# First feed-forward of a streaming-encoder block: token scalings in two steps, one plain feature tile instead of two, last middles stored from GpSimd's queue

## Chip, cores and metric

The kernel runs on one core of a Trainium2 chip. The metric is the device time of one execution in microseconds (us), smaller is better. The engines are named as in the profile: PE (TensorE matmuls), PEld (its weight loads), DVE (VectorE), ACT (ScalarE), POOL (GpSimd), SP (SyncE, which here only issues DMAs). "SPq", "ACTq" and "POOLq" are DMA issues on those engines' queues.

## What is computed

One encoder block over 16 meta tokens and 1024 frames (1040 tokens, 1024 model features, 2816 hidden features), in float32:

```python
def swiglu(x, w_gate, w_up, w_down):
    return (jax.nn.silu(x @ w_gate) * (x @ w_up)) @ w_down

h = jnp.concatenate([meta, x], axis=1)
h = h + 0.5 * swiglu(rmsnorm(h, ffn1_norm[l]), ffn1_w_gate[l], ffn1_w_up[l], ffn1_w_down[l])
u = rmsnorm(h, mix_norm[l])          # one projection, attention and gated linear attention, merge
h = h + mixed @ w_out[l]
h = h + 0.5 * swiglu(rmsnorm(h, ffn2_norm[l]), ffn2_w_gate[l], ffn2_w_up[l], ffn2_w_down[l])
return rmsnorm(h, final_norm)[:, N_META:]
```

The change touches the first feed-forward (the first line that updates `h`) and, in one helper, both.

## The kernel before

**Arithmetic.** Every float32 product is made of three matmuls over halves: each operand is cut into a rounded high half (an ACT copy) and the remainder as low half (a DVE subtraction), and high·high, high·low and low·high are accumulated in PSUM. `halves` (L228, L229) makes such a pair.

**Tokens.** The 1040 tokens stand as two halves c = 0 and 1 of 520 columns, each of two chunks; chunks q = 0 to 3 are 256, 264, 256 and 264 columns wide. Tokens are transposed on PE tile by tile (`xps`, L554 and L556), eight tiles m per chunk. Chunks 0 and 1 are put as they are, without the row scale 1/rms, which isn't known yet. For chunks 2 and 3 `second_put` copies the transposed tile out (ACT L581, `xr`, stored to DRAM for the residual), scales it (DVE L582, a scalar_tensor_tensor into `ub`), makes its high half (ACT L583) and, one put later, its low half (DVE L585). `rescale(m)` (L590) scales tile m of the first token half afterwards and makes its halves anew.

**Hidden features.** There are 22 tiles of 128 hidden features. Tiles 20 and 21 are made first, chunk by chunk (`head_products`, L631 to L633: 16 steps of three matmuls), while tokens arrive and are put. The order of this part is written by hand: `hooks[q, f]` names what stands between the steps of chunk q and head f, a step number before each. `out_of(f, q)` (`head_out`, L648 to L653) is SiLU times up of a head, in two pieces; `later` runs pieces that were set aside in `behind`. Then features 0 and 1 are made in the same plain way (`more`, 4 chunks x 16 steps x 3 = 192 matmuls each), with `finish` (L740, L741) as their SiLU times up. Meanwhile DVE makes the differences of tokens (`token_sums`, L246 to L252) and their halves, which the other features need. Features 2 to 19 go through `gate_ups`: a seven-product scheme for 2x2 blocks, 7 x 4 x 3 x 2 = 168 matmuls of 260 columns per tile (L453). A tile takes its seven combined results to DRAM (`f1mid`) with `keep` (L237 to L240): a cast to the high half `kh`, a subtraction to the low half `kl`, and a store of each.

**Down.** `down` runs the seven products over `f1mid`: it loads its moving tiles with `load_t` (L346, the first 14 from SP's queue, the others from ACT's), weights with `load_weights` (L358, SP), makes weight sums on POOL (`sums`, L436) and adds results up (ACT L395, DVE L340). The last tile's seven `keep`s are not needed at once and are taken one at a time during the first products of `down` (`pump`). There, with `self.ending` set, `kh` and `kl` lie in the ring `tmp` of four buffers, so a third pair waits until the first has been stored, the fourth for the second, and so on. The second feed-forward has the same code, and only two such `keep`s.

**Queues.** Engines run their own instructions in order; a DMA that is issued from an engine's queue stands in that order too. PSUM has eight banks for the plain products, two to a chunk (`pg`, `pu`); a chunk can start when the two banks are free again.

Of the kernel before, what the change touches and what calls it, by code (L numbers as in the profile page):

```python
# [8 lines left out]
F32 = mybir.dt.float32  # L9
# [10 lines left out]
KT = D // P  # L20
# [4 lines left out]
NF = DFF // P  # L25
# [10 lines left out]
def hybrid_kernel(  # L36
# [4 lines left out]
    nc = tc.nc  # L41
# [58 lines left out]
    def split(hi, lo, src):  # L100
        nc.scalar.copy(hi, src)
        nc.vector.tensor_sub(lo, src, hi.bitcast(F32))
# [49 lines left out]
    LAST = 2  # L152
# [16 lines left out]
    class Seven:  # L169
# [65 lines left out]
        def keep(self, dst, src):  # L235
            hi, lo = [ttile(x, F32R, self.n) if self.ending else self.block(x, F32R) for x in ("kh", "kl")]
            nc.scalar.copy(hi, src)  # L237
            nc.vector.tensor_sub(lo, src, hi.bitcast(F32))
            nc.sync.dma_start(out=dst[:, 0:self.n], in_=hi.bitcast(F32))
            nc.sync.dma_start(out=dst[:, self.n:], in_=lo.bitcast(F32))  # L240

        def token_sums(self, ub, between=None):

# [215 lines left out]
    N1 = T // 2  # L459
# [21 lines left out]
    ffn1 = Seven("f1", N1, acc1, (t_a, t_b, blk, s_pool, w_ext), ffn1_w_gate, ffn1_w_up, ffn1_w_down)  # L481
# [48 lines left out]
    B = [[None] * KT, [None] * KT]  # L530
# [44 lines left out]
    def second_put(q, m, ps):  # L575
        c, c0, n = CH[q]
        if c0 == 0:
            ub[1][m], B[1][m] = ffn1.block("ub"), ffn1.operand(False, "tb")
        raw = s_pool.tile([P, WB], F32, tag="s", name="xr")[:, 0:n]
        u, hi = ub[1][m][:, c0:c0 + n], B[1][m][:, c0:c0 + n]  # L580
        nc.scalar.copy(raw, ps)  # L581
        nc.vector.scalar_tensor_tensor(u, ps, vec[:, G1 + m:G1 + m + 1], racc[:, N1 + c0:N1 + c0 + n], op0=ALU.mult, op1=ALU.mult)  # L582
        nc.scalar.copy(hi, u)  # L583
        nc.sync.dma_start(out=x_dram[1, m, :, c0:c0 + n], in_=raw)
        return lambda: nc.vector.tensor_sub(B[1][m][:, N1 + c0:N1 + c0 + n], u, hi.bitcast(F32))  # L585

    def rescale(m):

        u = ub[0][m]
        nc.vector.scalar_tensor_tensor(u, u, vec[:, G1 + m:G1 + m + 1], racc[:, 0:N1], op0=ALU.mult, op1=ALU.mult)  # L590
        ffn1.halves(B[0][m], u)

    dgs = {}

# [25 lines left out]
    def head_products(q, ws, hooks, both=False):  # L620

        c, c0, n = CH[q]
        pss = [bank(x)[:, 0:n] for x in ("pg", "pu")]
        at = 0
        for i, k in [(i, k) for k in range(KT) for i in range(2)] if both else [(i, k) for i in range(2) for k in range(KT)]:
            for go in hooks.get(at, ()):
                go()
            at += 1
            wh, wl = [w[:, k * P:(k + 1) * P] for w in ws[i]]
            xh, xl = B[c][k][:, c0:c0 + n], B[c][k][:, N1 + c0:N1 + c0 + n]  # L630
            nc.tensor.matmul(pss[i], wh, xh, start=(k == 0), stop=False)  # L631
            nc.tensor.matmul(pss[i], wh, xl, start=False, stop=False)
            nc.tensor.matmul(pss[i], wl, xh, start=False, stop=(k == KT - 1))  # L633
        return pss
# [38 lines left out]
    def later():  # L673
        while behind:
            behind.pop(0)()
# [12 lines left out]
    def do(fn, *a, **k):  # L688
        return lambda: fn(*a, **k)
# [4 lines left out]
    def out_of(f, q):  # L694
        def go():
            rest = head_out(f, q, done.pop((f, q), None))
            later()
            behind.append(rest)
        return go

    turned = [turn_x(0, m) for m in range(KT)]
    for m in range(KT):
        first_put(0, m, turned[m])
        if m in (0, 3):
# [10 lines left out]
                 **{8 + m: [put(2, m)] for m in range(KT)}},  # L715
        (2, 0): {2: [emptied(1, 1)], 3: [out_of(0, 0)], **{4 + m: [put(3, m)] for m in range(KT)}, 13: [out_of(1, 0)]},
        (2, 1): {0: [out_of(0, 1)], 2: [out_of(1, 1)], 4: [out_of(0, 2)], 6: [later],
                 **{8 + m: [do(rescale, m)] for m in range(KT)}},
        (3, 0): {4: [out_of(1, 2)], 5: [later]},
        (3, 1): {4: [out_of(0, 3)], 5: [later]},  # L720
    }
    for q in range(4):
        for f in range(LAST):
            done[f, q] = head_products(q, heads[f], hooks[q, f], f == 0)
    manual.__exit__(None, None, None)
    ffn1.tops.update(B11=B[0][0:4], B21=B[0][4:8], B12=B[1][0:4], B22=B[1][4:8])
    out_c, ends = [[None] * 2 for _ in range(2)], []

    def more(f):

        ws = [ffn1.plain_weights(cols_view(w, f * P)) for w in (ffn1_w_gate, ffn1_w_up)]
        for q in (2, 3, 0, 1):
            c, c0, n = CH[q]
            pss = head_products(q, ws, {})

            def finish(c=c, c0=c0, n=n, pss=pss):
                a = ttile("a")[:, 0:n]
                if c0 == 0:
                    out_c[f][c] = ffn1.block("m0")
                nc.scalar.activation(a, pss[0], AF.Silu)  # L740
                nc.vector.tensor_mul(out_c[f][c][:, c0:c0 + n], pss[1], a)  # L741
            ends.append(finish)

    def between(n, k):
        for _ in range(2 if (n, k) in (("T2", 3), ("T1", 3), ("T3", 3), ("T4", 3)) else 0):
            ends.pop(0)()

    more(0)
    out_of(1, 3)()
    later()  # L750
    more(1)
    ffn1.token_sums(ub, between)
    turn_rest()
    for f in range(2):
        ffn1.middle(f, *out_c[f])
    ps_singles.close()
    dbl.update(down=False, a=ExitStack(), b=ExitStack())
    dbl["pools"] = [dbl[x].enter_context(tc.tile_pool(name=f"psd{x}", bufs=1, space=PSUM, side=side))
                    for x, side in (("a", "right"), ("b", "left"))]
    ffn1.gate_ups(range(2, NF - LAST))  # L760
    dbl["down"] = True
    ffn1.down(x_dram)
    mids, ws = ffn1.load_last(True)
# [66 lines left out]
    for c in range(2):  # L830
# [3 lines left out]
        for m in range(KT):  # L834
# [4 lines left out]
            n = 0  # L839
# [942 lines left out]
```

## Time and profile before

| | us |
|---|---|
| median of 3 runs | 2033.24 (2032.82 to 2035.1) |
| the profiled execution | 2034.17 |
| its span in the trace | 2032.5 |
| PE busy in it | 1999.0 |
| DVE / ACT / POOL busy in it | 1400.4 / 882.1 / 178.2 |

The span is what the trace shows from the first instruction to the last; the profiled execution's own time is 1.7 us more. Start times in the rows are counted from the span's start. A line of the trace's order of time has start, duration, engine, line, operation, output and inputs, and in square brackets how long the engine was idle before it and what ended that. In tables of stretches, PEclk is the granted TensorE clock as a share of full speed (1.00 is 2.4 GHz, 0.50 is 1.2 GHz).

### The profile page before, as it was taken

The page shows a single profiled execution, that of the slowest core. Times are in us where ns is not written, and L with a number is a line of the kernel's source. Part 1 is how long each engine was busy: PE and PEld are TensorE (multiplying, and loading weights), DVE is VectorE, ACT ScalarE, POOL GpSimd, SP SyncE. Part 2 cuts the span into 40 slices and gives each one's busy share as a digit, 9 for nine tenths or more (in the row PEclk, how much of TensorE's full clock was granted, in tenths as well). Part 3 has the DMA queues.
Part 4 walks back from the last instruction along what each step waited for, and adds up shares of the span by engine and source line. Part 5 has one row for each costly group of instructions (what it writes and reads, how often), then busy time and mean ns, then how long its engine had stood idle before and what let it go on. Part 6 is the DMA issues. An engine that isn't in the chain of part 4 may idle for free. (4 is left out here: it accounts for less than half of the span.)

```text
span 2032.5 us, 32056 instructions
## 1 busy us (share of the span) xinstructions
PE 1999.0 (98%) x12084; PEld 1776.5 (87%) x12084; DVE 1400.4 (69%) x2441; ACT 882.1 (43%) x1722; POOL 178.2 (9%) x205
## 2 busy tenths in 40 slices
PE   8899999999999999999999999999999999999998
PEld 8799999999899988888888767888888888878888
DVE  5866677667578776566367667568767767757885
ACT  5534444444322255465366535345444544442222
POOL 1000000001232100003200000110000000023212
PEclk9899999999999999999999999999999999999999
DMA  6324345438977143346222555741544544599722
GB/s 205 111 90 144 124 147 178 137 118 330 347 288 272 49 159 102 115 153 201 56 61 66 188 175 184 252 140 44 197 138 134 188 135 135 202 376 356 279 92 84
DMA packets 285772, 343.06 MB, mean 169 GB/s; under 512 B 26406, under 2 KB 192032, under 8 KB 285616
## 3 DMA queue, kind: packets, MB, share of 16 engines
q1 hardware_dynamic: 267968, 279.60, 41.5%
q10 hardware_dynamic: 17296, 61.29, 8.0%
q8 instruction: 95, 1.56, 0.3%
q14 instruction: 61, 0.50, 0.1%
q0 software_dynamic: 352, 0.11, 0.1%
HBM read 220.66 MB, written 120.27 MB: 168 GB/s over the span
## 5 line engine op out<-in xcount | busy, mean ns | idle before, releaser
L453 PE MATMUL pb<-tt,wop 128*128 128x260 f32 (+1 forms) x2208 | 383.9, 327 | 0.0
L453 PEld LDWEIGHTS pb<-tt,wop 128*128 128x128 f32 x2208 | 330.9, 188 | 35.5
L229 DVE TENSOR_TENSOR wop<-s,wop 128x512 fp32r<-128x512 f32 x264 | 186.8, 709 | 118.3 <-ACT wop L228 117.5
L228 ACT CAST wop<-s 128x512 fp32r<-128x512 f32 x264 | 163.7, 621 | 232.0 <-PE pb L453 96.0
L453 PE MATMUL pb<-tm,wop 128*128 128x260 f32 (+1 forms) x1440 | 235.9, 320 | 5.5 <-DVE h L340 3.3
L453 PEld LDWEIGHTS pb<-tm,wop 128*128 128x128 f32 x1440 | 208.6, 190 | 25.1 <-DVE h L340 3.7
L228 ACT CAST wop<-raw 128x512 fp32r<-128x512 f32 x198 | 122.9, 621 | 221.5 <-PE pb L453 108.3
L229 DVE TENSOR_TENSOR wop<-raw,wop 128x512 fp32r<-128x512 f32 x198 | 140.2, 710 | 30.1 <-ACT wop L228 29.8
L453 PE MATMUL pd<-tt,wop 128*128 128x260 f32 (+1 forms) x768 | 135.1, 329 | 0.0
L436 POOL TENSOR_TENSOR s<-raw 128x512 f32<-128x512 f32 x28 | 37.0, 1322 | 1054.6 <-DMA tm<-f1mid 455.1
L453 PEld LDWEIGHTS pd<-tt,wop 128*128 128x128 f32 x768 | 115.9, 188 | 13.1
L340 DVE SCALAR_TENSOR_TENSOR h<-pb,h 128x520 f32<-128x520 f32 (+1 forms) x136 | 93.9, 693 | 40.1 <-PE pb L453 38.0
L453 PE MATMUL pd<-tm,wop 128*128 128x260 f32 (+1 forms) x720 | 118.8, 319 | 0.0
L453 PE MATMUL pb<-tb,wop 128*128 128x260 f32 (+1 forms) x672 | 112.3, 320 | 0.5 <-ACT vec L87 0.5
L453 PEld LDWEIGHTS pd<-tm,wop 128*128 128x128 f32 x720 | 104.3, 188 | 9.3
L453 PE MATMUL pd<-tb,wop 128*128 128x260 f32 (+1 forms) x672 | 112.2, 320 | 0.0
L453 PE MATMUL pa<-tb,wop 128*128 128x260 f32 (+1 forms) x672 | 112.0, 320 | 0.0
L453 PEld LDWEIGHTS pb<-tb,wop 128*128 128x128 f32 x672 | 97.9, 188 | 9.9 <-ACT vec L87 0.6
L453 PEld LDWEIGHTS pd<-tb,wop 128*128 128x128 f32 x672 | 97.9, 188 | 9.3
L453 PEld LDWEIGHTS pa<-tb,wop 128*128 128x128 f32 x672 | 97.8, 188 | 9.3
L436 DVE TENSOR_TENSOR s<-raw 128x512 f32<-128x512 f32 x90 | 61.9, 688 | 54.6 <-DMA raw<-in_ffn_w_up 52.9
L340 DVE SCALAR_TENSOR_TENSOR h<-pd,h 128x520 f32<-128x520 f32 (+3 forms) x112 | 72.7, 655 | 33.3 <-PE pd L453 17.5
(410 smaller groups left out, 4036.8 us busy)
## 6 DMA issues: line engine op xcount, KB each, us to landing
tm<-f1mid ACTq DMA_DIRECT2D x56, 520.0 KB, 6.1
tm<-f2mid ACTq DMA_DIRECT2D x56, 512.0 KB, 6.0
raw<-in_ffn_w_gate SPq DMA_DIRECT2D x42, 512.0 KB, 3.8
raw<-in_ffn_w_up SPq DMA_DIRECT2D x42, 512.0 KB, 4.2
raw<-in_ffn_w_down SPq DMA_DIRECT2D x80, 256.0 KB, 5.2
f1mid<-kh SPq DMA_DIRECT2D x70, 260.0 KB, 3.2
f1mid<-kl SPq DMA_DIRECT2D x70, 260.0 KB, 3.4
f2mid<-kh SPq DMA_DIRECT2D x70, 256.0 KB, 2.9
```

The lines of the kernel that those rows point to most:

```text
L228: nc.scalar.copy(x[:, 0:n], src)
L229: nc.vector.tensor_sub(x[:, n:2 * n], src, x[:, 0:n].bitcast(F32))
L340: nc.vector.scalar_tensor_tensor(hm, ps, 0.5, hm, op0=ALU.mult, op1=ALU.add)
L436: (eng.tensor_add if add else eng.tensor_sub)(a[s], a[x], a[y])
L453: nc.tensor.matmul(ps, y, z[:, s0:s0 + sn], start=(first and k == 0 and at == 0), stop=(at == 2 and k == len(cols) - 1), skip_group_check= ...
```

## The change

It does four things.

1. `second_put` sets both halves of a scaled tile aside (`split` makes the pair), where before only the low one was. They run behind the next tile's copy and scaling.
2. `rescale` sets its halves aside too, and its eight calls are spread: four with two steps between them in chunk 2's second head, four with three steps between them in chunk 3's first head, with `out_of(1, 2)` ahead of these.
3. One tile of features goes the plain way, not two; features 1 to 19 go through the seven products. `out_of(1, 3)` and its second piece stand inside the plain tile, `finish` of a chunk is called at other places of `token_sums`.
4. While `ending` is set, `keep` issues its two stores from GpSimd's queue, not from SP's. In the first feed-forward that is 14 stores, in the second 4.

```diff
@@ keep
-            nc.sync.dma_start(out=dst[:, 0:self.n], in_=hi.bitcast(F32))
-            nc.sync.dma_start(out=dst[:, self.n:], in_=lo.bitcast(F32))
+            eng = nc.gpsimd if self.ending else nc.sync
+            eng.dma_start(out=dst[:, 0:self.n], in_=hi.bitcast(F32))
+            eng.dma_start(out=dst[:, self.n:], in_=lo.bitcast(F32))
@@ second_put
-        nc.scalar.copy(hi, u)
         nc.sync.dma_start(out=x_dram[1, m, :, c0:c0 + n], in_=raw)
-        return lambda: nc.vector.tensor_sub(B[1][m][:, N1 + c0:N1 + c0 + n], u, hi.bitcast(F32))
+        return lambda: split(hi, B[1][m][:, N1 + c0:N1 + c0 + n], u)
@@ rescale
-        ffn1.halves(B[0][m], u)
+        later()
+        behind.append(lambda: ffn1.halves(B[0][m], u))
@@ hooks
         (2, 1): {0: [out_of(0, 1)], 2: [out_of(1, 1)], 4: [out_of(0, 2)], 6: [later],
-                 **{8 + m: [do(rescale, m)] for m in range(KT)}},
-        (3, 0): {4: [out_of(1, 2)], 5: [later]},
-        (3, 1): {4: [out_of(0, 3)], 5: [later]},
+                 **{8 + 2 * m: [do(rescale, m)] for m in range(4)}},
+        (3, 0): {4: [out_of(1, 2)], **{6 + 3 * i: [do(rescale, 4 + i)] for i in range(4)}},
+        (3, 1): {0: [later], 4: [out_of(0, 3)], 5: [later]},
@@ more, between
-            pss = head_products(q, ws, {})
+            pss = head_products(q, ws, hooks if q == 2 else {})
-        for _ in range(2 if (n, k) in (("T2", 3), ("T1", 3), ("T3", 3), ("T4", 3)) else 0):
+        if (n, k) in (("T2", 1), ("T2", 3), ("T1", 3), ("T3", 3)):
             ends.pop(0)()
-    more(0)
-    out_of(1, 3)()
-    later()
-    more(1)
+    more(0, {4: [out_of(1, 3)], 5: [later]})
     ffn1.token_sums(ub, between)
-    for f in range(2):
-        ffn1.middle(f, *out_c[f])
+    ffn1.middle(0, *out_c)
-    ffn1.gate_ups(range(2, NF - LAST))
+    ffn1.gate_ups(range(1, NF - LAST))
```

The order on ACT where chunk 3 is put. Before (`xr` is the copy out of PSUM, `tb` a high half; tiles m follow one another):

```order
L581 COPY xr_683<-xps_679 128x264
L583 CAST tb_552<-ub_551 128x264
L652 CAST kept_116<-a_672 128x256
L581 COPY xr_697<-xps_693 128x264
L583 CAST tb_565<-ub_564 128x264
```

In the changed kernel, the same place:

```order
L582 COPY xr_683<-xps_679 128x264
L653 CAST kept_116<-a_671 128x256
L582 COPY xr_696<-xps_692 128x264
L101 CAST tb_552<-ub_551 128x264
L582 COPY xr_709<-xps_705 128x264
L101 CAST tb_564<-ub_563 128x264
```

The cast of tile m (`tb_552`) stood ahead of the copy of tile m+1 and now stands behind it.

The order on DVE at the end of the rescalings. Before (`a_907` is SiLU times up of head 1, chunk 2, `out_of(1, 2)`; `ub_230` and `ub_235` are tiles 6 and 7 of the first token half; L246 to L248 are token differences):

```order
L590 SCALAR_TENSOR_TENSOR ub_230<-ub_230,vec_84,racc_115 128x520
L248 TENSOR_TENSOR ub_620<-ub_620,ub_201 128x520
L246 TENSOR_TENSOR ub_206<-ub_578,ub_206 128x520
L229 TENSOR_TENSOR tb_231<-ub_230,tb_231 128x520
L590 SCALAR_TENSOR_TENSOR ub_235<-ub_235,vec_84,racc_115 128x520
L247 TENSOR_TENSOR ub_578<-ub_634,ub_578 128x520
L246 TENSOR_TENSOR ub_211<-ub_592,ub_211 128x520
L229 TENSOR_TENSOR tb_236<-ub_235,tb_236 128x520
L649 TENSOR_TENSOR a_907<-pu_801,a_907 128x256
```

In the changed kernel (`a_893` is the same SiLU times up, `ub_211` is tile 3, `ub_220` tile 4):

```order
L590 SCALAR_TENSOR_TENSOR ub_211<-ub_211,vec_84,racc_115 128x520
L229 TENSOR_TENSOR tb_207<-ub_206,tb_207 128x520
L650 TENSOR_TENSOR a_893<-pu_801,a_893 128x256
L229 TENSOR_TENSOR tb_212<-ub_211,tb_212 128x520
L590 SCALAR_TENSOR_TENSOR ub_220<-ub_220,vec_84,racc_115 128x520
L654 TENSOR_TENSOR kept_119<-a_893,kept_119 128x256
L590 SCALAR_TENSOR_TENSOR ub_225<-ub_225,vec_84,racc_115 128x520
```

The reading of chunk 2's banks for head 1 (`pu_801`) moved from behind the eighth rescaling, and token differences among them, to between the fourth and the fifth; no token difference stands ahead of it any more.

SP's queue at the start of `down`, before (`tm` are moving tiles of `f1mid`, `kh` and `kl` the halves of the last tile, `raw2` weights):

```order
L346 DMA tm_5913<-f1mid_104 128x1040
L346 DMA tm_5915<-f1mid_104 128x1040
L239 DMA f1mid_104<-kh_5965 128x520
L240 DMA f1mid_104<-kl_5966 128x520
L239 DMA f1mid_104<-kh_6003 128x520
L240 DMA f1mid_104<-kl_6004 128x520
L358 DMA raw2_6196<-in_ffn1_w_down 128x2x256 x2
L358 DMA raw2_6199<-in_ffn1_w_down 128x2x256 x2
L239 DMA f1mid_104<-kh_6041 128x520
```

The same stores in the changed kernel, on POOL (`s` are weight sums; the first pair, `kh_5956`, stands right ahead of these rows):

```order
L437 TENSOR_TENSOR s_6109<-raw_5885 128x512
L437 TENSOR_TENSOR s_6111<-s_6109,raw_5882 128x512
L437 TENSOR_TENSOR s_6113<-raw_5882,raw_5885 128x512
L437 TENSOR_TENSOR s_6115<-raw_5882,s_6111 128x512
L240 DMA f1mid_104<-kh_5994 128x520
L241 DMA f1mid_104<-kl_5995 128x520
L240 DMA f1mid_104<-kh_6032 128x520
L241 DMA f1mid_104<-kl_6033 128x520
L240 DMA f1mid_104<-kh_6103 128x520
L241 DMA f1mid_104<-kl_6104 128x520
L437 TENSOR_TENSOR s_6376<-raw2_6190 128x512
L240 DMA f1mid_104<-kh_6148 128x520
```

The stores left SP's queue, where 14 loads of `tm` stood ahead of the first, and now share POOL's order with the weight sums.

## Rows read from the trace of the kernel before

**Rows 1.** The page, its first part: busy time, share of the span, instructions.

```profile
PE 1999.0 (98%) x12084; PEld 1776.5 (87%) x12084; DVE 1400.4 (69%) x2441; ACT 882.1 (43%) x1722; POOL 178.2 (9%) x205
```

**Rows 2.** PE's waits over the span: total us, times, longest.

```profile
PE pg L631 <- ACT a L648: 7.1, 1, 7.1
PE pb L453 <- DVE h L340: 3.3, 1, 3.3
...
PE pb L453 <- ACT h L395: 2.2, 2, 1.5
PE xps L554 <- DVE ub L582: 2.1, 5, 0.7
...
PE pa L453 <- ACT h L395: 0.9, 1, 0.9
```

**Rows 3.** Table of stretches (start and end us); its first line names the columns.

```profile
core 0: us, PE busy (x) PEld busy (x) DVE busy (x) ACT busy (x) POOL busy (x), PEclk, DMA share, GB/s
...
57.80:61.30 3.50, 3.50 (x19) 3.50 (x19) 2.31 (x6) 1.82 (x7) 0.00 (x0) 0.52 0.33 109
...
84.20:91.50 7.30, 0.21 (x2) 0.01 (x1) 7.30 (x13) 2.16 (x4) 0.00 (x0) 0.80 0.34 98
91.50:95.60 4.10, 4.07 (x19) 4.07 (x20) 4.10 (x10) 2.86 (x8) 0.00 (x0) 0.52 0.00 0
...
110.80:133.90 23.10, 23.10 (x194) 23.00 (x192) 7.19 (x13) 5.84 (x12) 0.00 (x0) 1.00 0.08 24
200.00:300.00 100.00, 100.00 (x837) 100.00 (x836) 65.76 (x103) 43.15 (x75) 0.00 (x0) 1.00 0.39 128
...
520.00:525.00 5.00, 3.19 (x16) 3.19 (x17) 3.82 (x6) 1.70 (x4) 1.29 (x1) 0.71 1.03 372
```

**Rows 4.** Order of time, 51.9 to 54.3 us: puts of chunk 3.

```profile
51.94 0.48 DVE L582 SCALAR_TENSOR_TENSOR ub<-xps,vec,racc 128x256 f32<-128x256 f32 x1 [0.41 <-ACT xr L581]
...
52.45 0.41 ACT L583 CAST tb<-ub 128x256 fp32r<-128x256 f32 x1 [0.55 <-DVE ub L582]
...
53.36 0.23 PE L554 MATMUL xps<-ident,x 16*128 16x16 f32 x1
...
54.24 0.23 PE L554 MATMUL xps<-ident,x 16*128 16x16 f32 x1
```

**Rows 5.** Order of time, ACT before PE's longest wait; DVE within the plain tile.

```profile
90.57 0.62 ACT L228 CAST tb<-ub 128x520 fp32r<-128x520 f32 x1 [1.88 <-DVE ub L590]
...
120.58 2.54 DVE L229 TENSOR_TENSOR tt<-ub,tt 128x520 fp32r<-128x520 f32 x4 [3.44 <-ACT tt L228]
```

**Rows 6.** Order of time, 483 to 521 us: SP's queue.

```profile
483.57 16.29 SPq L346 DMA_DIRECT2D tm<-f1mid  x10
...
513.22 0.41 SPq L239 DMA_DIRECT2D f1mid<-kh  x1
...
520.06 0.32 SPq L239 DMA_DIRECT2D f1mid<-kh  x1
```

**Rows 7.** Order of time, 511 to 527 us: ACT's casts of the kept tile.

```profile
511.85 0.63 ACT L237 CAST kh<-tm 128x520 fp32r<-128x520 f32 x1 [0.56 <-DMA f1mid<-kh]
...
519.41 0.62 ACT L237 CAST kh<-u 128x520 fp32r<-128x520 f32 x1 [4.87 <-DMA f1mid<-kh]
...
526.23 0.62 ACT L237 CAST kh<-g 128x520 fp32r<-128x520 f32 x1 [2.17 <-DMA f1mid<-kh]
```

**Rows 8.** DMA issues, 497 to 530 us: count, KB each, median us to landing.

```profile
tm<-f1mid ACTq DMA_DIRECT2D x7, 520.0 KB, 6.2
...
tm<-f1mid SPq DMA_DIRECT2D x3, 520.0 KB, 11.5
```

**Rows 9.** Tile kh, 470 to 535 us: its 11 stores of 260 KB.

```profile
DMA to landing us min/median/max: 4.2/5.4/10.9
```

**Rows 10.** DMA issues, 760 to 780 us, columns as in rows 8.

```profile
gk_dram<-g SPq DMA_DIRECT2D x2, 128.0 KB, 1.8
gwf<-in_gla_gate_w POOLq DMA_DIRECT2D x6, 16.0 KB, 4.1
```

More of the change, by code (lines that the diff above doesn't have):

```diff
@@ L726, in hybrid_kernel, with more @@
     ffn1.tops.update(B11=B[0][0:4], B21=B[0][4:8], B12=B[1][0:4], B22=B[1][4:8])
-    out_c, ends = [[None] * 2 for _ in range(2)], []
-    def more(f):
+    out_c, ends = [None] * 2, []
+    def more(f, hooks):
         ws = [ffn1.plain_weights(cols_view(w, f * P)) for w in (ffn1_w_gate, ffn1_w_up)]
@@ L738, in finish @@
                 if c0 == 0:
-                    out_c[f][c] = ffn1.block("m0")
+                    out_c[c] = ffn1.block("m0")
                 nc.scalar.activation(a, pss[0], AF.Silu)
-                nc.vector.tensor_mul(out_c[f][c][:, c0:c0 + n], pss[1], a)
+                nc.vector.tensor_mul(out_c[c][:, c0:c0 + n], pss[1], a)
             ends.append(finish)
     def between(n, k):
-        for _ in range(2 if (n, k) in (("T2", 3), ("T1", 3), ("T3", 3), ("T4", 3)) else 0):
+        if (n, k) in (("T2", 1), ("T2", 3), ("T1", 3), ("T3", 3)):
             ends.pop(0)()
-    more(0)
-    out_of(1, 3)()
-    later()
-    more(1)
+    more(0, {4: [out_of(1, 3)], 5: [later]})
     ffn1.token_sums(ub, between)
     turn_rest()
-    for f in range(2):
-        ffn1.middle(f, *out_c[f])
+    ffn1.middle(0, *out_c)
     ps_singles.close()
```

## The prediction

> **What bounds the kernel now.** The page's first part comes first: PE is busy 1999.0 of the span's 2032.5 us, 98% [rows 1]. So a change can gain in three ways: fewer matmul columns, less idle time of PE, and fewer matmuls at the lower clock. The second view is the list of PE's waits [rows 2]. The reader should see that a few waits hold most of the idle time and that each has a place: one of 7.1 us (a plain chunk's banks, waiting for a SiLU on ACT), five that sum to 2.1 us (token transposes, waiting for DVE's scaling), and in `down` 3.3 (DVE L340), 0.9 and, of the 2.2 in two, 0.7 (the longest, 1.5, is that of the second feed-forward). The third view is the table of stretches [rows 3], for the granted clock: behind the transposes' waits it shows 0.52, behind the 7.1 us also 0.52, behind the one of 3.3 us 0.71, and 1.00 in undisturbed stretches. 0.52 is nearly the lower of the two levels (1.2 against 2.4 GHz), so each cluster of waits costs a second time.
>
> **Part 1, the puts.** Per put, DVE's scaling (0.48 us) waits for ACT's copy, and ACT's cast stands idle 0.55 us for that scaling before it runs (0.41) [rows 4]; the next copy stands behind the cast. So ACT and DVE take turns. PE's own pace between two puts is 0.88 us (53.36 to 54.24, where it didn't wait) [rows 4]. In the changed order the copy of the next tile stands ahead of the cast, so neither engine waits for the other within a put. DVE then has the scaling and the low half, 0.48 and about 0.41 (taken like the cast of the same size), 0.89 together and a little less as neighbours overlap; ACT has a copy and a cast, about 0.8. Both fit PE's 0.88, so I take all 2.1 us of the five waits [rows 2]. What is late next is nothing by more than 0.01 us a put. The clock: 57.8 to 61.3 us has 19 matmuls, two of them ends of the transposes, so 17 in 3.5 us. At full clock one takes 23.1 / 192 = 0.120 [rows 3], 17 take 2.0. That returns 1.5. Sum **3.6**.
>
> **Part 2, the rescalings.** In 84.2 to 91.5 us DVE is busy 7.30 of 7.30 while PE has nearly nothing (0.21) [rows 3]. PE waits for banks that the SiLU of `out_of(1, 2)` on ACT (L648) and its product on DVE must read first. In the order of before both stand behind all eight rescalings; ACT sits at a high half until DVE has rescaled (1.88 us idle) [rows 5], and DVE takes token differences in between. In the changed order four rescalings and no difference stand ahead of that reading. Four rescalings and four low halves, at the 7.30 / 13 = 0.56 of that stretch, are 4.5 us of DVE, spread over eight steps of PE (8 x 3 x 0.120 = 2.9 us) and a little more; so the banks are read within a chunk (16 x 3 x 0.120 = 5.8 us) and the first feature tile, one chunk later, finds them free. I take the whole 7.1 us. Behind it 19 matmuls took 4.1 us at 0.52 [rows 3] where 19 x 0.120 = 2.3 would do: 1.8. Sum **8.9**.
>
> **Part 3, one plain tile fewer.** A plain tile is 192 matmuls, 23.1 us (110.8 to 133.9); in the steady stretch a matmul takes 100 / 837 = 0.1195 us [rows 3], and the seven-product tile has 168, that is 20.1. Gain **3.0**. The extra tile's work on DVE and ACT (busy 65.8 and 43.2 in 100 us of such tiles) is hidden behind PE. But the plain tile that goes was cover: DVE has to finish 16 token differences and sums, 16 low halves (2.54 / 4 = 0.64 each [rows 5], and the differences taken alike) and the four products of `finish` (0.4, as in the puts) before the third product of feature 1: 20.5 + 1.6 = 22.1 us. It can begin when the rescalings and the two last SiLUs of the heads are done, some 3 us behind the start of the plain tile: chunk 2's first head ends at about 61.0, near the end of the stretch at 0.52 [rows 3], so at 57.4 after part 1, and three chunks of 48 matmuls later (17.3 us) it is 74.7. With one weight cut behind it that is about 101; the third product's matmuls are due at 74.7 + 23.1 + 2 x 24 x 0.120 = 103.6. Both are estimates from these durations. DVE also has weight cuts and sums to do in between, about 1 us: a cover of about 1.5 us. It is costed at nothing; without that cover each microsecond is lost (rival 3).
>
> **Part 4, the last stores.** Seven pairs of 260 KB are stored through a ring that holds two pairs. Before, the first pair's stores stood on SP behind ten loads whose issue took from 483.57 to 499.9 [rows 6]. From then on one chain decides: the third pair's cast at 511.85, its store issued at 513.22, landed when the fifth pair's cast starts, 519.41; that store issued at 520.06, landed for the seventh's cast at 526.23 [rows 6, 7]. Each landing is 6.2 us. Behind these casts stand the additions on ACT and DVE that PE waits for (3.3 and 0.9).
> In the changed order the first pair is stored at once, so the third cast loses its 0.56 us of waiting [rows 7], and its store is issued at its end, not 0.74 us later. What a store of 260 KB takes from POOL's queue no row shows. From below: in this stretch loads of 520 KB landed in 6.2 us from ACT's queue and in 11.5 from SP's, which held far more [rows 8]; half the size would be 3.1. From above: POOL's loads of 16 KB landed in 4.1 us where SP's stores of 128 KB landed in 1.8 [rows 10], so POOL's queue may add 2.3: to the 6.2 of now that makes 8.5. I take 3.1 + 2.3 = 5.4, since a queue of its own and POOL's addition are both in the rows; 5.4 is also the median of kh's stores [rows 9]. Then the fifth cast starts at 511.3 + 0.6 + 5.4 = 517.3, 2.1 earlier, and the seventh at 517.3 + 0.6 + 5.4 = 523.3, 2.9 earlier. PE gets 2.1 of the 3.3, then 0.8 of the 0.9. The clock is taken as unchanged, as a wait of 1.2 stays. Gain **2.9**.
> The Trainium skill, "DMA: Bandwidth & Descriptors", section "Anatomy of one DMA", gives about 2.0 us and bytes / 436 GB/s for a transfer from GpSimd's queue, 2.6 us here. By that figure the chain would be gone and this part would give 6.2; no row shows such a transfer in a full stretch, and the loads of 16 KB at 4.1 us speak against it.
> POOL's own queue: ahead of its weight sums now stand stores that wait for casts. The sum that waited for weights until the second step's weights had landed now stands behind the fourth pair's store, and its weights no longer behind stores on SP; the next sum stands behind the sixth's. Weight cuts, and so PE, wait for these sums; I cost that at nothing, because the casts that they stand behind come 2 us earlier. In the second feed-forward only two pairs are kept and no chain of landings forms; its wait of 1.5 [rows 2] is left as it is: 0, with -1.5 to +1 as bounds.
>
> **Sum.** 3.6 + 8.9 + 3.0 + 2.9 = 18.4 us. Against the profiled execution's 2034.17 that is 2015.8; the median is 0.93 below that execution, so **2014.8**.
>
> **Rivals.**
> 1. *Stores from POOL land fast.* At 3.1 us the third pair is gone before the fifth needs its place. Then all of 3.3 + 0.9 + 0.7 and the clock of 520 to 525 (16 matmuls in 3.19 us [rows 3] for 1.9: 1.3) come back, 6.2. For it: ACT's queue against SP's [rows 8]. Against: POOL's small loads [rows 10]. Time: 2033.24 - 15.5 - 6.2 = **2011.5**. The Trainium skill, "DMA: Bandwidth & Descriptors", section "Queues, rings and completion order", has an engine take turns between the queues it has work for; by that, a store on a third queue would not stand behind SP's loads.
> 2. *Stores from POOL land later.* At 8.5 us the fifth cast starts at 520.4 and the seventh at 529.5, 3.3 later than now. 2033.24 - 15.5 + 3.3 = **2021.0**. The Trainium skill, "SBUF — State Buffer", section "SBUF: two separate sides", says that GpSimd cannot write a transfer's descriptors while some DVE operations hold a shared port; no row of this case shows such a hold.
> 3. *The plain tile's cover is missed.* Each of the 16 halves may cost DVE a turn with ACT as in the puts, 0.55 [rows 4]: 8.8, less the 1.5 of cover, 7.3. It decides from 1.5 us of delay on, and a wait of PE at feature 1 takes the place of the 7.1. 2014.8 + 7.3 = **2022.1**.
> 4. *Slower than before.* The chain of two landings eats all the rest. It decides from 5.4 + 18.4 / 2 = 14.6 us per landing; the slowest of eleven stores took 10.9 [rows 9]. At 15.5 the sum is 20.2 later: **2035.0**.
> 5. *The puts' pace doesn't change*, because the scaling still waits for the copy and the copy for a transposed tile: 3.6 not gained, **2018.4**.
>
> **How the numbers follow.** The forecast has 0.41 (its own range 2013 to 2017), rival 1 0.21, rival 2 0.13, rival 3 0.14, rival 4 0.05, rival 5 0.06. The range reaches to rival 1 with 1 us for the second feed-forward and to rivals 2 and 3: 2010.5 to 2022.5. What lies beyond is rival 4, the stronger forms of 2 and 3, and a stall or two more than the sum holds. About 4 us, 0.2%, can be told from no change here; of rival 4, 0.01 lies within that, 0.04 beyond. All else is faster: 0.95.
>
> **What would show it.** Part 1: no wait of PE on L583's scaling, granted clock near 1.00 where it was 0.52, and chunk 2's second head starting at about 57.4. Part 2: no wait of several us on a plain chunk's banks, the plain tile running at about 0.120 per matmul. Part 3: 192 fewer and 168 more matmuls, and no wait of PE within feature 1's first products (rival 3 otherwise). Part 4: the landing of `f1mid<-kh` from POOLq: about 5.4, 3.1 or 8.5, and with it a PE wait behind L340 of about 1.2, none or over 4. Wrong it would be if PE's waits went but the span fell by less: then the clock is what I misread.

## The result and the profile after

| | before | changed |
|---|---|---|
| median, us | 2033.03 (4 runs, 2032.82 to 2035.1) | 2017.94 (4 runs, 2016.82 to 2024.48) |
| the profiled execution, us | 2034.17 | 2016.82 |
| its span, us | 2032.5 | 2015.1 |

The ratio is 0.9927, 95% interval 0.9909 to 0.9944: 15.1 us faster by the medians, where 18.4 was forecast; the time lies 3.1 us above the forecast and inside the range. The changed kernel's profiled execution is the fastest of its four, and the one of before was above its median, so the two spans differ by more, 17.4 us. A second set of six runs of the changed kernel, beside the experiments, gave 2019.01 (2015.64 to 2025.07) and the ratio 0.9929 (0.9911 to 0.9946). Single executions of it spread over some 10 us, so differences of 1 or 2 us between kernels are read below from stretches of the traces, not from medians. The kernel before ran again beside each of the three sets of experiments: its medians there were 2035.83 (11 runs), 2032.59 (17) and 2033.70 (11). The ratios below go by the set's own runs of it.

The page of the changed kernel, first part, against [rows 1]:

```profile
PE 1989.4 (99%) x12060; PEld 1767.3 (88%) x12060; DVE 1408.7 (70%) x2451; ACT 886.5 (44%) x1728; POOL 187.9 (9%) x223
```

PE is busy 9.6 us less, 24 matmuls fewer (192 less 168) and fewer of them at the low clock; the other 7.8 us of the span were idle time of PE. Its waits, against [rows 2] (total us, times, longest):

```profile
PE pb L454 <- ACT h L396: 3.4, 2, 3.1
PE xps L557 <- DMA x<-in_x: 3.1, 1, 3.1
PE pb L454 <- DMA tm<-f2mid: 1.6, 1, 1.6
...
PE pb L454 <- DVE m L742: 0.7, 1, 0.7
...
PE pb L454 <- DVE h L341: 0.4, 1, 0.4
```

The wait of 7.1 us on a plain chunk's banks is gone, and so are the five on DVE's scaling. In the first `down` the 3.3 us behind DVE's addition are 0.4 and the 0.9 behind ACT's are gone; but a wait on ACT's addition that was 0.65 before is 3.1 now, and one of 1.6 us on a load stands in the second `down`. Stretches of the changed kernel, columns as in [rows 3]: the start, the two heads of chunk 2, the first two chunks of the plain tile, the first seven-product tile, and `down`:

```profile
20.00:30.00 10.00, 8.74 (x66) 7.57 (x65) 8.12 (x16) 5.63 (x14) 3.20 (x2) 1.00 1.01 334
45.80:61.40 15.60, 15.60 (x123) 14.31 (x122) 14.98 (x39) 13.05 (x34) 0.00 (x0) 1.00 0.45 164
73.10:84.60 11.50, 11.50 (x99) 11.50 (x98) 11.50 (x22) 5.54 (x12) 0.00 (x0) 1.00 0.39 139
97.20:117.20 20.00, 20.00 (x167) 20.00 (x168) 15.89 (x25) 9.60 (x17) 0.00 (x0) 1.00 0.28 81
480.00:520.00 40.00, 36.47 (x289) 36.06 (x288) 24.76 (x31) 17.32 (x32) 17.52 (x20) 0.96 0.99 364
```

In the second to fourth line PE is busy throughout, and the granted clock is 1.00 (2.4 GHz). Note DVE in the third line, 11.50 of 11.50: the work didn't shrink, PE no longer waits for it.

The puts, in order of time, against [rows 4]:

```profile
52.12 0.42 DVE L102 TENSOR_TENSOR tb<-ub,tb 128x264 fp32r<-128x264 f32 x1
52.24 0.41 ACT L101 CAST tb<-ub 128x264 fp32r<-128x264 f32 x1
52.46 0.49 DVE L583 SCALAR_TENSOR_TENSOR ub<-xps,vec,racc 128x264 f32<-128x264 f32 x1
52.56 0.37 ACT L582 COPY xr<-xps 128x264 f32<-128x264 f32 x1
52.86 0.42 DVE L102 TENSOR_TENSOR tb<-ub,tb 128x264 fp32r<-128x264 f32 x1
...
53.20 0.49 DVE L583 SCALAR_TENSOR_TENSOR ub<-xps,vec,racc 128x264 f32<-128x264 f32 x1
```

No row has an idle time before it: a put takes 0.74 us (52.46 to 53.20) where two casts of before stood 1.23 apart.

The first `down`: PE's wait, ACT's rows around it, a kept pair's cast, and the landing of transfers in 480 to 515 us:

```profile
495.79 2.97 PE L454 MATMUL pb<-tm,wop 128*128 128x260 f32 x12 [3.14 <-ACT h L396]
...
506.57 1.70 PE L454 MATMUL pb<-tm,wop 128*128 128x260 f32 x12 [0.39 <-DVE h L341]
```
```profile
494.76 0.33 ACTq L347 DMA_DIRECT2D tm<-f1mid  x1
495.14 0.60 ACT L396 ACTIVATE h<-pb 128x520 f32<-128x520 f32 x1 [7.65 <-DMA tm<-f1mid]
...
502.12 0.63 ACT L237 CAST kh<-u 128x520 fp32r<-128x520 f32 x1 [3.31 <-DMA f1mid<-kh]
```
```profile
tm<-f1mid ACTq DMA_DIRECT2D x8, 520.0 KB, 7.2
tm<-f1mid SPq DMA_DIRECT2D x4, 520.0 KB, 12.8
f1mid<-kh POOLq DMA_DIRECT2D x6, 260.0 KB, 5.7
f1mid<-kl POOLq DMA_DIRECT2D x6, 260.0 KB, 6.0
```

The third pair's store was issued at 497.04 from POOL and the fifth pair's cast began at 502.12: a landing of 5.1, and 5.7 by the median, near the 5.4 that the prediction took. The fifth pair's store, the chain's second link, took only 2.9 (503.05 to 505.97). The fifth cast came at 22.6 us from the start of `down` (479.5), against 22.4 before (519.41 less 497.0): the chain of stores did not end earlier, because the third cast stood behind ACT's late addition. ACT had stood 7.65 us in front of a load on its own queue. That load waited for one that SP had issued at 481.87 and that landed at 494.74; it went out at 494.76. Of SP's load the trace says who waited for it, and how long it took to land:

```profile
  ACT h L396: 7.6, 1
DMA to landing us min/median/max: 12.9/12.9/12.9
```

The same load stood in the same place in the kernel before, and PE lost less behind it:

```profile
510.84 1.70 PE L453 MATMUL pb<-tm,wop 128*128 128x260 f32 x12 [0.65 <-ACT h L395]
```

There it was released 12.7 us from the start of `down` (509.75 less 497.05), in the changed kernel 15.3 us.

### The profile page after: what moved, and what is told of

Same layout as the page of the kernel before. It is cut to its first block, busy times and chain, and to the rows that moved or that the text cites. A ratio compares the mean times of both kernels' runs of the same rounds, so it can differ in the third digit from the quotient of the medians.

```text
span 2015.1 us, 32030 instructions
## 1 busy us (share of the span) xinstructions
PE 1989.4 (99%) x12060; PEld 1767.3 (88%) x12060; DVE 1408.7 (70%) x2451; ACT 886.5 (44%) x1728; POOL 187.9 (9%) x223
## 4 chain that ended last, share of the span: by engine, by line
PE 88%; DMA 5%; DVE 3%; issue 1%; ACT 1%; POOL 0%; SPq 0%; DVEq 0%; ACTq 0%; POOLq 0%
PE pb L454 35%; PE pd L454 17%; PE pa L454 9%; PE pj L96 2%; PE pj L97 2%; PE pj L98 2%; PE wo L96 1%; PE wo L97 1%; PE wo L98 1%; PE pd L841 1%; DMA tm<-f2mid 1%; PE pj L929 1%; PE pj L930 1%; PE pj L931 1%; DMA tm<-f1mid 1%
## 5 line engine op out<-in xcount | busy, mean ns | idle before, releaser
L454 PE MATMUL pb<-tt,wop 128*128 128x260 f32 (+1 forms) x2280 | 393.0, 326 | 0.0
L454 PEld LDWEIGHTS pb<-tt,wop 128*128 128x128 f32 x2280 | 339.8, 188 | 35.5
L454 PEld LDWEIGHTS pb<-tm,wop 128*128 128x128 f32 x1440 | 208.2, 189 | 25.3 <-ACT h L396 4.1
L229 DVE TENSOR_TENSOR wop<-raw,wop 128x512 fp32r<-128x512 f32 x201 | 144.7, 721 | 29.7 <-ACT wop L228 29.5
L454 PEld LDWEIGHTS pd<-tt,wop 128*128 128x128 f32 x792 | 118.9, 188 | 13.1
L341 DVE SCALAR_TENSOR_TENSOR h<-pd,h 128x520 f32<-128x520 f32 (+3 forms) x112 | 72.5, 654 | 31.5 <-PE pd L454 16.1
```

The lines of the kernel that those rows point to most:

```text
L229: nc.vector.tensor_sub(x[:, n:2 * n], src, x[:, 0:n].bitcast(F32))
L341: nc.vector.scalar_tensor_tensor(hm, ps, 0.5, hm, op0=ALU.mult, op1=ALU.add)
L454: nc.tensor.matmul(ps, y, z[:, s0:s0 + sn], start=(first and k == 0 and at == 0), stop=(at == 2 and k == len(cols) - 1), skip_group_check= ...
```

## Experiments

The stretches that the verdicts use, from the starts of PE's matmuls in each trace, in us: A, start of chunk 1's first head; B, chunk 2's two heads; C, the plain tile's first two chunks (with the wait on the banks); D, from the first product of the first `down` to the projections; E, from the last tile of the second gate and up to the end of its `down`.

| kernel | A | B | C | D | E | median (runs) |
|---|---|---|---|---|---|---|
| before | 32.7 | 19.6 | 20.7 | 454.4 | 208.6 | 2033.03 (4) |
| changed | 31.3 | 15.6 | 11.5 | 452.6 | 209.2 | 2017.94 (4) |
| changed, again | 30.9 | 15.6 | 11.5 | 453.4 | 209.2 | 2019.01 (6) |
| u1_puts | 32.6 | 19.6 | 16.0 | 452.9 | 210.5 | 2026.09 (5) |
| u2_rescale | 31.1 | 15.6 | 13.3 | 453.4 | 210.3 | 2020.25 (5) |
| u3_plain | 31.5 | 15.6 | 11.5 | 453.7 | 209.8 | 2022.41 (6) |
| u4_stores | 31.3 | 15.6 | 11.5 | 454.4 | 210.7 | 2019.16 (5) |
| w1_only_puts | 33.0 | 15.6 | 13.1 | 454.3 | 208.4 | 2024.99 (5) |
| w2_only_rescale | 31.6 | 18.1 | 16.5 | 454.7 | 208.5 | 2029.25 (12) |
| v1_load_behind | 30.8 | 15.6 | 11.5 | 451.9 | 209.2 | 2017.07 (6) |
| v2_load_gpsimd | 30.9 | 15.6 | 11.5 | 455.0 | 206.7 | 2018.49 (5) |
| v3_load2_gpsimd | 31.2 | 15.6 | 11.5 | 451.9 | 208.2 | 2017.52 (5) |
| v4_pump | 31.5 | 15.6 | 11.5 | 455.8 | 210.3 | 2020.31 (6) |
| v5_load_pump | 31.3 | 15.6 | 11.5 | 456.3 | 207.1 | 2018.32 (5) |

### One part undone: u1 to u4

**u1_puts**: the puts as before, all else changed.

```diff
+        nc.scalar.copy(hi, u)
         nc.sync.dma_start(out=x_dram[1, m, :, c0:c0 + n], in_=raw)
-        return lambda: split(hi, B[1][m][:, N1 + c0:N1 + c0 + n], u)
+        return lambda: nc.vector.tensor_sub(B[1][m][:, N1 + c0:N1 + c0 + n], u, hi.bitcast(F32))
```

> The changed kernel with only the puts as before: the high half's cast right behind the scaling, ahead of the next copy. Theory (the terms add up, each at its own place): ACT and DVE take turns again, five waits of PE on the scaling, some 2.1 us in all, and a stretch at about 0.5 of full clock behind them, 3.6 together: 2021.5 against 2017.9 of the changed kernel. Rival (the 5.5 us by which chunk 2's second head starts earlier in the changed kernel's trace are all due to the puts): 2023.4. Rival (the granted clock there is chance and not the waits' doing): 2020.0.

Measured 2026.09, ratio to before 0.9956 (0.9941 to 0.997): some 8 us above the changed kernel by the medians, 6 by the ratios, and 8.6 in the stretches B and C, where the theory had 3.6 and the larger rival 5.5. B has 4.0 more, near the 3.6. C has 4.5 more, which weren't expected: PE waits for DVE in another place. From u1's trace:

```profile
81.60 0.58 PE L635 MATMUL pg<-tb,wlo 128*128 128x256 f32 x1 [2.74 <-DVE wlo L216]
```

DVE is late with the cut of the plain tile's weights (`wlo`, the low half). The slow puts make DVE late, and what they delay isn't paid for at their own place alone.

**u2_rescale**: the rescalings and the hooks as before, all else changed.

```diff
-        later()
-        behind.append(lambda: ffn1.halves(B[0][m], u))
+        ffn1.halves(B[0][m], u)
-                 **{8 + 2 * m: [do(rescale, m)] for m in range(4)}},
-        (3, 0): {4: [out_of(1, 2)], **{6 + 3 * i: [do(rescale, 4 + i)] for i in range(4)}},
-        (3, 1): {0: [later], 4: [out_of(0, 3)], 5: [later]},
+                 **{8 + m: [do(rescale, m)] for m in range(KT)}},
+        (3, 0): {4: [out_of(1, 2)], 5: [later]},
+        (3, 1): {4: [out_of(0, 3)], 5: [later]},
```

> The changed kernel with only the rescalings as before: eight in a row in chunk 2's second head, halves at once, the SiLU of chunk 2's second head behind them. Theory: PE waits about 7 us for the banks of a plain chunk, behind ACT's SiLU, with 1.8 us more at the lower clock: 8.9, so 2026.8. Rival (the wait came from the token differences on DVE, which in the changed kernel follow the one plain tile's weights and no longer mix with the rescalings): under 3 us, 2020 to 2021.

Measured 2020.25, ratio 0.9929 (0.9915 to 0.9944): 1 to 2 us above the changed kernel, not 9. The wait on the banks is there, at the same place and behind the same SiLU, but short:

```profile
80.23 0.39 PE L631 MATMUL pg<-tb,whi 128*128 128x264 f32 x1 [1.50 <-ACT a L648]
```

So with the fast puts the old rescalings cost 1.8 in C. The theory's 8.9 for this part fell. The rival's number (2020 to 2021) came true, but its reason fell: in this kernel's order on DVE the token differences stand between the rescalings as before.

**u3_plain**: two plain tiles and 18 seven-product tiles.

```diff
-    more(0, {4: [out_of(1, 3)], 5: [later]})
+    more(0, {4: [out_of(1, 3)], 5: [later]})
+    more(1, {})
-    ffn1.gate_ups(range(1, NF - LAST))
+    ffn1.gate_ups(range(2, NF - LAST))
```

> The changed kernel with two plain tiles and 18 seven-product tiles again. Theory: 24 more matmuls net, 23.1 less 20.1 is 3.0, less the 0.7 us of waiting for the plain tile's last product that the longer cover takes away: 2.3 to 2.7, so 2020.4. Rival (the cover of the second plain tile is worth more, since DVE's chain is late in some executions): 2018 or less.

Measured 2022.41, ratio 0.9941 (0.9925 to 0.9957). The medians put it 3 to 4 us above the changed kernel, with a spread (2018.39 to 2025.07) that can't settle tenths. The traces can: from the end of C to feature 2's first product it takes 35.4 us; in the changed kernel 12.6 to feature 1's first product and 20.1 for that tile, 32.7. That is 2.7; the changed kernel's wait of 0.7 on the plain tile's last product is in it, and in u3's a wait of 0.5 at the same place. The theory holds; the rival doesn't.

**u4_stores**: the last pairs' stores on SP's queue, all else changed.

```diff
-            eng = nc.gpsimd if self.ending else nc.sync
+            eng = nc.sync
```

> The changed kernel with the last tile's stores on SP's queue again. Theory: the chain of two landings comes back with its waits (3.3 on DVE's addition, 0.9 on ACT's) and the wait of 3.1 us on ACT's addition that the changed kernel's trace has at 495.8 us goes: between the start of the down products and the projections behind it 2.0 us more, 2019.9. Rival (one wait only took the other's place): 2017.9, no difference. Rival (stores on GpSimd's queue cost time elsewhere, in the second down): 2016 to 2017.5.

Measured 2019.16, ratio 0.9921 (0.9906 to 0.9936): no difference from the changed kernel that its runs can show. In D it is 454.4, as all four kernels with stores on SP (454.3 to 454.7), where the six traces with stores, loads and casts in the first `down` as in the changed kernel (v3 below among them) have 451.9 to 453.7: 1.5 us by the means. The long wait is again that of before, behind the chain of landings, and a bit longer:

```profile
504.55 5.57 PE L454 MATMUL pb<-tm,wop 128*128 128x260 f32 x24 [3.74 <-DVE h L341]
```

The wait of 3.1 us is 0.3 here, and u4 differs from the changed kernel in this edit alone. In the four kernels with stores on SP, the SP load that ACT's load waits for takes 11.1 to 12.2 us to land and ACT's load is released 11.3 to 12.7 us from the start of `down`; in the eight traces with stores on POOL and loads on ACT it is issued up to 2.9 us later, takes 12.8 to 13.2 us and releases ACT's load at 14.4 to 15.9. PE's wait behind it is at most 0.65 in the former and 2.3 to 3.7 in the latter; wherever PE waits, the wait is the time of the release less 12.1 to 12.3 us. So the stores' move made most of this wait. It stands some 10 us ahead of the chain's.

E is 210.7 without GpSimd's stores. PE's one wait there is 2.1 us (1.5 before), and behind it the granted clock falls to 0.65 over 1806 to 1810 us; in E it is 1.00 in all the other traces.

### One part alone: w1 and w2

u1 and u2 together say that parts 1 and 2 work on one wait. These two make either change on the kernel before.

> The kernel before with the change of the puts alone. Theory by now (parts 1 and 2 pull at the same wait: DVE is some 8 us behind PE when the rescalings begin, and either fewer microseconds of lag or the earlier SiLU frees the banks): the puts give 4.0 at their own place and cut the long wait on a plain chunk's banks from 7.1 to 1.5 to 4, since DVE starts the rescalings 5 us earlier against PE; 9 to 11 in all, 2022 to 2024. Rival (the sum of the prediction, each part at its own place): 3.6 in all and the wait of 7 us still there, 2029.5.

> The kernel before with the spread rescalings and halves in two steps alone. Theory by now: the wait on the banks goes from 7.1 to about 2.7 and ends on DVE's cut of the plain tile's weights rather than on ACT's SiLU, since DVE is still late by what the puts cost; 4 to 5 gained, 2028 to 2029. Rival (the sum of the prediction): the whole wait and its clock, 8.9 gained, 2024.

w1 measured 2024.99, ratio 0.9958 (0.9946 to 0.997); w2 2029.25, ratio 0.9979 (0.9968 to 0.9989). Both lie within 1 us of where the common wait puts them (2022 to 2024, and 2028 to 2029), and not where the sum of the prediction had them (2029.5 and 2024). Against before in their own set, w1 gains 7.6 by the medians, less than its B and C (11.6); where the rest went isn't shown. In w1 the wait on the banks is 1.3 us, C is 7.6 shorter than before:

```profile
81.91 0.39 PE L630 MATMUL pg<-tb,whi 128*128 128x264 f32 x1 [1.32 <-ACT a L647]
```
```profile
60.39 0.76 DVE L589 SCALAR_TENSOR_TENSOR ub<-ub,vec,racc 128x520 f32<-128x520 f32 x1
```

The second row is w1's first rescaling. It starts 3.0 us behind the start of chunk 2's second head (57.4). In the kernel before that distance is 7.9, from 61.05:

```profile
68.99 0.75 DVE L590 SCALAR_TENSOR_TENSOR ub<-ub,vec,racc 128x520 f32<-128x520 f32 x1
```

DVE's lag of 5 us, made by the puts, was most of the wait of 7.1. In w2 the wait has another cause, as in u1:

```profile
79.53 0.38 PE L634 MATMUL pg<-tb,wlo 128*128 128x256 f32 x1 [3.22 <-DVE wlo L216]
```

C over the four combinations: 20.7 (neither), 13.1 to 13.3 (puts alone), 16.0 to 16.5 (rescalings alone), 11.5 (both). The puts take 7.4 to 7.6 of it alone and 4.5 to 5.0 as the second step; the rescalings 4.1 to 4.7 alone and 1.6 to 1.8 as the second.

w2 tells the cost of the puts' waits and of the clock apart. It has the five waits of 2.1 us in all, and yet the clock stays at 1.00:

```profile
46.00:64.20 18.20, 16.10 (x123) 14.42 (x122) 11.95 (x30) 10.64 (x29) 0.00 (x0) 1.00 0.27 91
```

B is 18.1 there, 2.5 above 15.6; where the clock fell too, in the kernel before and in u1, it is 19.6, another 1.5. So the fall needs more than these waits to come about; what else isn't known.

The column A: in four of fourteen traces (before, u1, u3, w1) the granted clock is 0.83 over 20 to 30 us, in ten 1.00, while all kernels have the same order of instructions up to there. w1's row, against the changed kernel's above:

```profile
20.00:30.00 10.00, 8.75 (x53) 7.63 (x53) 7.50 (x13) 5.04 (x13) 3.23 (x2) 0.83 0.94 307
```

In three of the four, A is 32.6 to 33.0, in u3 31.5 like the others. w1 has the new puts and the fall, w2 the old ones and no fall: it isn't the puts' doing. 1.4 us of the 17.4 between the two profiled spans are this.

### The wait in the down products: v1 to v5

**v1_load_behind** puts the load that ACT issues in a step behind the additions of that step:

```diff
-                    if 0 < kg < NG:
-                        self.load_t(kg, ts[kg], at, nc.scalar)
                     ...
                             self.add_half(self.by_parts(self.h[m][c]), pss[j])
+                    if 0 < kg < NG:
+                        self.load_t(kg, ts[kg], at, nc.scalar)
```

**v2_load_gpsimd** issues these loads with `nc.gpsimd` instead of `nc.scalar`.

> The changed kernel with each load that ACT issues during the down products put behind ACT's and DVE's additions of that step, not ahead of them. Theory (the wait of 3.1 us at 495.8 us comes from a load on ACT's queue that waits for an earlier load from SP's queue to land, with the additions queued behind it): that wait goes, 3 to 4.5 us with the clock behind it, 2013.5 to 2015. Rival (the additions are late because PE or DVE is late): no difference, 2018. Rival (the loads come later, and PE waits for them): 2019 or more.

> The changed kernel with these loads issued from GpSimd's queue, where the last stores are too. Theory (as for the load put behind): ACT issues no loads and waits for none, the 3.1 us go; 2013.5 to 2015. Rival (the loads now stand behind stores and weight sums on POOL and land later): PE waits for its moving tiles, 2019 to 2024.

v1: 2017.07, ratio 0.9923 (0.991 to 0.9935). v2: 2018.49, ratio 0.9925 (0.9913 to 0.9937). Neither differs from the changed kernel, and neither reaches the 2013.5 to 2015 of its theory. v1 still has the wait, for the load now stands ahead of the next step's additions:

```profile
493.44 0.33 ACTq L347 DMA_DIRECT2D tm<-f1mid  x1
493.82 0.60 ACT L394 ACTIVATE h<-pb 128x520 f32<-128x520 f32 x1 [6.83 <-DMA tm<-f1mid]
```
```profile
494.47 1.70 PE L454 MATMUL pb<-tm,wop 128*128 128x260 f32 x12 [2.32 <-ACT h L394]
```

v2 has no load on ACT, and the wait is gone. So the load on ACT's queue was its cause. In the written order that load waits on the same completion counter (the semaphore that tells of a landing) as SP's load of 481.87, and the trace has it go out 0.02 us behind that load's landing; v1 has the same pair of times (landing at 493.42, issue at 493.44). But in v2 the chain of stores, which the earlier wait had covered, is back:

```profile
506.25 4.66 PE L454 MATMUL pb<-tm,wop 128*128 128x260 f32 x24 [3.10 <-DVE h L341]
514.45 1.71 PE L454 MATMUL pa<-tm,wop 128*128 128x260 f32 x12 [2.10 <-ACT h L396]
```
```profile
tm<-f1mid POOLq DMA_DIRECT2D x6, 520.0 KB, 10.0
```

The third pair's store, now on one queue with the loads, took 10.4 us to land there, against 5.0 in the changed kernel. D is 455.0, 2 us longer than with the loads on ACT. E, where two pairs make no chain, is 206.7, 2.5 shorter, and has no wait of PE.

**v3_load2_gpsimd** therefore moves only the second feed-forward's loads (`eng_t = nc.scalar if self is ffn1 else nc.gpsimd`). **v4_pump** takes the kept pairs later, `if slot in (0, 1, 3, 5, 7, 9, 11)` in place of `(0, 1, 2, 4, 5, 7, 8)`. **v5_load_pump** is v2 with v4. The changed kernel itself ran beside them.

> The changed kernel itself, as the measure for the three beside it and for a second profile. Theory: 2017 to 2019, the clock's fall at 22 to 27 us is there or not by chance (1.4 us), and the wait on ACT's addition in the first down products is there again, about 3 us. Rival (the fall at the start belongs to the slow puts): again none.

> The changed kernel with the moving tiles of the second feed-forward's down loaded from GpSimd's queue, those of the first from ACT's as they are. Theory (a load on ACT's queue that waits for an earlier transfer holds the additions behind it, and in the second down no chain of stores takes its place): the waits of 1.6 and 0.3 there go, 2 to 2.5 us, 1.2 per thousand less than the changed kernel. Rival (they only shift into the weights' loads): no difference.

> The changed kernel with the last seven pairs taken at steps 0, 1, 3, 5, 7, 9, 11 of the down products, not at 0, 1, 2, 4, 5, 7, 8. Theory (the chain of landings costs PE 0.4 to 0.9, and the wait of 3 us behind the load on ACT stays): no more than 1 us less. Rival (ACT's lateness at that wait comes from the casts of the pairs): 3 us less. Rival (the tiles that hold the pairs come free later and the additions wait for them): 2 us more or worse.

> The changed kernel with both: all moving tiles of the down products loaded from GpSimd's queue and the pairs taken at steps 0, 1, 3, 5, 7, 9, 11. Theory (with no loads on ACT, what was left was the chain of landings, 3.1 and 2.1 us; later steps give each landing two more products' time): 4 to 6 us less than with the loads alone, 2012 to 2014. Rival (the chain is bound by the landings themselves wherever the casts stand): 2017 to 2019.

Medians 2019.01, 2017.52, 2020.31 and 2018.32, ratios 0.9929 (0.9911 to 0.9946), 0.9921 (0.9906 to 0.9937), 0.9943 (0.9922 to 0.9964) and 0.9924 (0.9908 to 0.9939). The changed kernel has its wait again (3.73 us at 496.06) and no fall of the clock at the start. v3 has a shorter E (208.2), without the waits for loads and ACT's additions, and D as in the changed kernel; but from E to the end of the span it takes 45.4 us where the others take 43.5 to 44.0, and 1.5 us of median are inside the spread of the runs: a lead, not a proof. The theories for v4 and v5 were wrong: D is 455.8 and 456.3, longer than the changed kernel's and v2's; the times fit rivals of theirs (2 us more; 2017 to 2019). In v5 PE waits longer for the same chain, not less:

```profile
506.65 2.97 PE L454 MATMUL pb<-tm,wop 128*128 128x260 f32 x12 [5.07 <-DVE h L341]
...
517.91 3.19 PE L454 MATMUL pd<-tm,wop 128*128 128x260 f32 x24 [1.53 <-DVE h L341]
```

Four placings of loads and stores give four different longest waits in the first 40 us of `down` (0.7, 3.3 and 0.9 before; 3.1 and 0.4 in the changed kernel; 3.1 and 2.1 in v2; 5.1 and 1.5 in v5), and PE loses 3.5 to 6.6 us by them each time. The DMA engines are busy 0.99 of that stretch in the changed kernel. That the transfers' amount sets the time there, and the order only where the wait shows, is what this suggests; no run here took transfers away.

## Why the prediction was right, and where not

**Part 1, its own place: right.** Forecast 3.6, measured 4.0 in B; no wait on the scaling is left and the clock is 1.00. Chunk 2's second head starts at 55.7; from 57.4 that is the 1.4 of chance at the start and 0.3.

**Part 2: the sum right by luck, the cause wrong.** Forecast 8.9, and C with the clock behind it is 9.2 shorter. But the step by which ACT's SiLU stands behind eight rescalings, so that moving it ends the wait, left out why DVE was so late there. u2 and w1 show that the fast puts alone take 7.4 to 7.6 us of C, and that the rescalings' new place adds only 1.6 to 1.8. The two terms added up correctly because both changes were made together. Rival 5 (the puts' pace stays) was priced at 3.6; u1's stretches show 8.6, since the terms weren't independent.

**Part 3: right.** Forecast 3.0, measured 2.7 (35.4 less 12.6 and 20.1), the same against the kernel before and against u3. The cover held but for a wait of 0.7 in place of one of 0.5. Rival 3 did not happen.

**Part 4: the term that was mis-sized.** Forecast 2.9; D gives 1.9 between the two profiled executions and 1.5 by the means over ten traces. The price of a landing was right for the chain's first link (5.4 taken, 5.1 measured, 5.7 by the median) and too high for the second (2.9). What failed is the step "From then on one chain decides", which took the chain of landings as the only thing late and the stores' effect on the other queues' loads at nothing: with the stores on POOL, SP's loads land later, and an ACT load that waits for one of them holds ACT's additions. That wait went from 0.65 to 3.14 us, and this took back 2.5 of the 3.8 us that PE gained at the chain (3.26 and 0.93 less 0.39). The prediction asked what POOL's queue would hold up, and not what ACT's did; the 0.7 that it read in its list of waits was this load. By rival 1 the waits should have gone with a fast landing, by rival 2 they should have grown with a slow one; neither has this wait.

The Trainium skill, "DMA: Bandwidth & Descriptors", section "Anatomy of one DMA", gives a fit by which such a store would take 2.6 us, an estimate. Measured in a stretch with the DMA engines full it is 5.7 by the median, and the measurement decides. Of the hold that "SBUF — State Buffer" of the Trainium skill describes, in its section "SBUF: two separate sides", no row shows anything: kh's stores took a median of 5.7 from POOL and 6.3 from SP in u4.

**The second `down`, taken at 0 with -1.5 to +1 as bounds: 0.7 lost.** E is 208.4 to 208.6 in before, w1 and w2, and 209.2 in both traces of the changed kernel. In the seven traces with stores on POOL and loads on ACT there, PE waits 1.2 to 2.2 us for a load of `tm`, and all its waits in E sum to 1.9 to 2.9, against 1.4 to 1.5 in before, w1 and w2. SP's last load of the first group takes 13.9 to 14.1 us to land in the seven, and 10.9 to 11.7 in the four kernels with stores on SP, u4 among them, which have no such wait. So part 4 makes this wait too. u4's long E is another matter, the fall of the clock named there.

**The sum.** 4.0 + 9.2 + 2.7 + 1.5 - 0.7 = 16.7, where the forecast had 18.4: part 4 gave 1.4 less, the second `down` 0.7 less, part 3 0.3 less, parts 1 and 2 0.7 more. The medians have 15.1. The 1.6 between lie outside these stretches; single executions spread more than that, and what made them isn't shown. The profiled execution of before also contained the fall of the clock at its start, 1.4 us, which the change could not remove.

## What to carry to other kernels

An engine that is late at one place delivers its lag at the next: before a wait is credited to the instructions that stand ahead of it, look how far behind that engine already is when it comes to them. Moving transfers to another queue makes those on the old queue land at other times, so for each wait that is to go, read every queue at that place for what is issued there and waits for a landing, loads on compute engines too. An earlier wait covers a later one: the load's wait here covered the chain, which came back when the loads left ACT. Where the DMA engines are full, moving transfers between queues moved the wait more than the time.

## What the runs showed of the hardware

- The granted clock at the start fell to 0.83 over 20 to 30 us in four of fourteen traces and not in ten, with the same order of instructions; and five waits of together 2.1 us came with a fall in the kernel before and in u1, and without one in w2. The same waits of PE don't always have the same price: 2.5 us or 4.0.
- In the full stretch of the first `down`, a load of 520 KB landed in 7.2 us from ACT's queue, 12.8 from SP's and, in v2, 10.0 from POOL's (medians); the stores of 260 KB took 5.7 and 6.0 from POOL, and 6.3 and 6.4 from SP in u4. In v2, with the loads on POOL too, two of them took 10.3 and 10.4.
- An issue on ACT's queue that waited for another transfer's landing held ACT's own work for 7.65 us. With stores on POOL and not on SP, the SP load behind this landed in 12.8 to 13.2 us and not in 11.1 to 12.2.
- Issuing a store from POOL took 0.54 to 0.59 us of POOL each; with 18 stores that is the 9.7 us by which POOL is busier (178.2 to 187.9).
